# One of five dense token blocks computed mixed: gathered dots on VectorE during the front, its weights through the gate matrices into the dense second stage

## The chip, the cores and the metric

The kernel runs on one core of a Trainium2 chip. TensorE (PE in the profile, PEld for its weight loads) multiplies matrices, VectorE (DVE) and ScalarE (ACT) work elementwise, GpSimd (POOL) does elementwise work and issues the indirect transfers, SyncE (SP) issues most other transfers. The metric is the device time of one execution in microseconds (us), as the median of several runs; lower is better.

## The reference, cut to what matters

The input is 1024 tokens of 1024 features, f32. A mixer (mLSTM heads and gated MLP groups) adds to the residual x; then a PEER layer looks up 16 of 16384 single-neuron experts for each of 8 heads of each token:

```python
q = (xt @ w_query).reshape(T, PEER_HEADS, 2, PEER_HALF)
s = jnp.einsum('thpd,hpkd->thpk', q, sub_keys)
...                     # top 16 of each half, top 16 of their sums: idx and gate (T, 8, 16)
ub = jnp.take(expert_u, ib, axis=0)      # per block of 128 tokens
vb = jnp.take(expert_v, ib, axis=0)
a = jax.nn.gelu(jnp.einsum('td,thkd->thk', xb, ub))
return jnp.einsum('thk,thkd->td', a * gb, vb)
```

So every token has 128 picks: a dot product with a row of `u` for each, a gelu, a gate, and a weighted sum of rows of `v`. A final RMSNorm follows.

## The kernel before, in words

The tokens are 8 blocks of 128. The PEER layer treats them in two ways.

**Dense blocks 0 to 4** (`DENSE`, line 28). All 16384 experts are computed for all 640 tokens, 128 experts (one expert row) at a time. Stage 1 (`stage1` in `experts`, lines 768 to 791) multiplies the row of `uT` with the transposed activations `xh`/`xl`; every product is made of three float32r matmuls of high and low halves (`mm3`, lines 89 to 96). With 8 chunks of 128 features and two halves of 320 tokens that is 48 matmuls of 320 columns for one row. ACT applies the gelu (L786), DVE multiplies with the gate matrix `Gin` (L788), ACT and DVE split the result into `wh` and `wl` (L789, L790). Stage 2 (`stage2`, lines 793 to 814) runs once per group of four rows (`GS`): for each of 5 blocks and 2 halves of the features it accumulates 12 matmuls of 512 columns into `pout`, and DVE adds that to `acc` (L814). POOL makes the low halves of `u` and `v` (L779, L801), ACT the high ones (L778, L800). There are 32 groups.

The gate matrices are made ahead, by `gate_units` (lines 641 to 666): 32 "quads" a block, each one compare on DVE (L656), four scaled copies on ACT (L659), four f32 matmuls (L661, each is two records) and a copy out on ACT (L662); every eighth quad stores 2 MB to `d_G`. Stage 1 reads `d_G` back once per group as `Gin` (one buffer, L771).

**Sparse blocks 5 to 7** (`SPARSE`). For each block `sparse_units` gathers one row of `u` per token with an indirect transfer (POOL, L693) and takes its dot product on DVE (L697), 128 times; then the same with rows of `v`, added into an accumulator (L709, L713). That is 768 gathers of 512 KB. They go into 4 buffers `gat` and, in the dense part, 3 more under the tag `AB`. Their instructions are emitted between the expert rows of the dense loop, in even portions (`SPREAD`, line 833).

**The front** (`front_part`) makes everything ahead of that, in three parts of 2, 3 and 3 blocks (`PARTS`): mixer, output projection, the normalised activations (high and low halves of the dense blocks stored to `d_xh`, `d_xl`, and loaded in `open_x`), the queries and scores. Top-k work (`topk_units`) and gate matrices of one part's blocks are side work of the next part: `interleave` emits it among the steps of `front_part`, spread over the first 210 of a nominal 332 units (`FTOT`). So the gate matrices of blocks 0 and 1 are side work of part 1, those of blocks 2 to 4 of part 2.

**What sets the order.** The kernel is written in Tile. A simulated timeline at build time gives each engine one fixed instruction order, by priority (`first()` raises some evictions) and expected readiness; on the chip each engine and each DMA queue takes its instructions strictly in that order, with semaphore waits. Gathers in the dense part are held in program order on POOL (`keep_in_program_order`).

Of the kernel before, what the change touches and what calls it, by code (L numbers as in the profile page):

```python
# [18 lines left out]
D = 1024  # L19
# [7 lines left out]

DENSE = [0, 1, 2, 3, 4]
SPARSE = [5, 6, 7]
GS = 4  # L30
# [9 lines left out]
NRAW = 3  # L40
NGAT = 4
SLOW = 0
# [4 lines left out]
class Build:  # L47
# [405 lines left out]
    def topk_units(self, blk):  # L453
# [15 lines left out]
        def merge(h0):  # L469
            ijg = st["ijg"]  # L470
            self.merge16(h0, st["tv"], st["ti"], ijg)
            if blk in self.sparse:
                if h0 == 0:
                    self.pick[blk] = (self.kp.tile([128, 128], I32, name="ix", tag=f"ix{blk % 2}"),
                                      self.kp.tile([128, 128], F32, name="gt", tag=f"gt{blk % 2}"))
                ix, gt = self.pick[blk]
                hl = slice(h0 * 16, (h0 + HB) * 16)
                v.scalar_tensor_tensor(ix[:, hl], ijg[:, 0, hl], float(NEXP), ijg[:, 1, hl], op0=OP.mult, op1=OP.add)
                v.tensor_copy(gt[:, hl], ijg[:, 2, hl])

        def done():
            ijg = st["ijg"]
            if blk in self.dense:
                pt = self.gps.tile([128, 3, 128], F32, name="pG", tag="pG", bufs=2)
                for k in range(3):
                    nc.tensor.transpose(pt[:, k], ijg[:, k], self.ident)
                t = self.gp.tile([128, 3, 128], F32, name="ijgT", tag="ijgT", bufs=1)
                nc.scalar.activation(t, pt, AF.Copy)
                self.pick[blk] = t
# [68 lines left out]
    def front_part(self, part):  # L558
# [115 lines left out]


    def sparse_units(self, blk, pool, psum):

# [3 lines left out]
        def begin():  # L681
            st["ix"], st["gt"] = self.pick[blk]
            st["xn"] = psum.tile([128, D], F32, name="xn", tag="xn", bufs=1)
# [54 lines left out]
    def open_x(self):  # L738

        nc = self.nc  # L740
        self.cm.close()
        self.xp = self.ctx.enter_context(self.tc.tile_pool(name="xparts", bufs=1, side="right", reuse_waits="tile"))
        T = len(self.dense) * 128
        self.xh = self.xp.tile([128, 8, T], F32R, name="xh", tag="xh")
        self.xl = self.xp.tile([128, 8, T], F32R, name="xl", tag="xl")
        for s, blk in enumerate(self.dense):
            for src, dst in ((self.d_xh, self.xh), (self.d_xl, self.xl)):
                nc.sync.dma_start(dst[:, :, s * 128:(s + 1) * 128].bitcast(F32), src[blk])
# [7 lines left out]
    def experts(self, side, dp, ps):  # L756
# [4 lines left out]
        ND = len(self.dense)  # L761
        T = ND * 128
        T2 = T // 2
        n32 = T // TG
        ngroups = NEXP // GS
        W, V, st = {}, {}, {"n": 0}

        def stage1(g, e):
            if e == 0:
                st["G"] = dp.tile([128, n32, GS, TG], F32, name="Gin", tag="Gin", bufs=1)  # L770
                nc.sync.dma_start(st["G"], self.d_G[:, :, g * GS:(g + 1) * GS].rearrange("n j i t -> j n i t"))  # L771
            G = st["G"]
            i = g * GS + e
# [7 lines left out]
            wl = dp.tile([128, T], F32R, name="wl", tag="wl", bufs=GS + 1)  # L781
            for s in range(2):
                pa = ps.tile([128, T2], F32, name="pa", tag="pa", bufs=3)
                sl = slice(s * T2, (s + 1) * T2)
                self.mm3(pa, [((uh[:, c], ul[:, c]), (xh[:, c, sl], xl[:, c, sl])) for c in range(8)])
                nc.scalar.activation(pa, pa, AF.Gelu_apprx_tanh)  # L786
                p3 = pa.rearrange("p (n t) -> p n t", t=TG)
                v.tensor_tensor(p3, p3, G[:, s * (n32 // 2):(s + 1) * (n32 // 2), e], op=OP.mult)  # L788
                nc.scalar.activation(wh[:, sl], pa, AF.Copy)  # L789
                v.tensor_sub(wl[:, sl], pa, wh[:, sl].bitcast(F32))  # L790
            W[i] = (wh, wl)

        def stage2(g):
# [9 lines left out]
            for s in range(ND):  # L803
                for d in range(2):
                    if st["n"] % 3 == 0:
                        po = ps.tile([128, 512], F32, name="pout", tag="pout", bufs=1)
                    else:
                        po = self.gps.tile([128, 512], F32, name="pout", tag="pG", bufs=2)
                    st["n"] += 1
                    dl = slice(d * 512, (d + 1) * 512)  # L810
                    sl = slice(s * 128, (s + 1) * 128)
# [51 lines left out]
    def side_units(self, b0, nb):  # L863

        side, prev = [], []
        for blk in range(b0, b0 + nb):
            if blk in self.dense:
                if blk != b0:
                    side += merged(prev, self.topk_units(blk))
                prev = self.gate_units(blk)  # L870
        return side + prev

    def run(self):
        tc = self.tc
        ND = len(self.dense)
        with ExitStack() as ctx:
# [13 lines left out]
            self.kp = ctx.enter_context(tc.tile_pool(name="keep", bufs=1))  # L890
            self.pick = {}
            self.ctx = ctx
# [104 lines left out]
```

## Time and profile before

| | us |
|---|---|
| median of 3 runs | 2883.05 (2881.18 to 2901.98) |
| profiled execution | 2879.65 |
| its span, first to last instruction | 2877.8 |
| part 0 of the front, about | 0 to 228 |
| part 1, about | 228 to 585 |
| part 2, about | 585 to 985 |
| dense loop, with the sparse blocks inside it | 1005 to 2820 |
| end | 2820 to 2878 |

The parts are read from the first and last instructions of lines that belong to one step (the load of x at 230 and 560, the query evictions up to 976, the first stage 1 at about 1000). Of 2877.8 us PE is busy for 2708.7, DVE 2195.1, POOL 1501.2 and ACT 1120.9. A busy share is no rate: matmul records overlap, so the pace of PE is read from the distance between the starts of two matmuls.

### The profile page before, as it was taken

The numbers are of one execution on the slowest core, as the hardware profiler recorded it, in microseconds if no ns is written. First come the engines' busy times: TensorE is split into PE (matmuls) and PEld (weight loads), VectorE is DVE, ScalarE is ACT, GpSimd is POOL, SyncE is SP. The second block draws the span as 40 slices with busy tenths as digits, with TensorE's granted clock in tenths as the row PEclk, the third lists the DMA queues.
The fourth block names the chain that finished last, engine by engine and source line by source line (L and its number), as shares of the span: only waits on it lengthen the run. The fifth ranks groups of instructions, "written<-read, shape, count | busy, mean of one in ns | idle before, by whom it ended". The sixth has DMA issues, their size and how long they took to land.

```text
span 2877.8 us, 44768 instructions
## 1 busy us (share of the span) xinstructions
PE 2708.7 (94%) x16283; PEld 2470.3 (86%) x16283; DVE 2195.1 (76%) x4981; ACT 1120.9 (39%) x2295; POOL 1501.2 (52%) x1220
## 2 busy tenths in 40 slices
PE   7888989999898799999989999999999999999998
PEld 7887989889898798888878889889888899888987
DVE  6649975289985677888887787978987777777774
ACT  5444788348888332223222222223222232222222
POOL 3430010000100186777766677767767777768772
PEclk9989999999999899999999999999999999999999
DMA  7798557866578798998988999998889999989992
GB/s 245 256 313 281 188 211 280 276 223 225 187 272 302 264 326 300 323 336 306 333 288 304 336 321 331 308 342 308 309 280 331 344 327 332 334 314 332 326 345 95
DMA packets 327821, 838.41 MB, mean 291 GB/s; under 512 B 25520, under 2 KB 161072, under 8 KB 315824
## 3 DMA queue, kind: packets, MB, share of 16 engines
q0 software_dynamic: 114048, 427.87, 40.2%
q1 hardware_dynamic: 190544, 347.91, 37.5%
q10 hardware_dynamic: 23008, 59.77, 5.3%
q8 instruction: 128, 2.10, 0.3%
q14 instruction: 93, 0.76, 0.1%
HBM read 746.32 MB, written 89.13 MB: 290 GB/s over the span
## 4 chain that ended last, share of the span: by engine, by line
PE 58%; DVE 17%; DMA 9%; issue 6%; ACT 4%; POOL 4%; SPq 1%; ACTq 1%; POOLq 0%; DVEq 0%
PE pa L96 7%; PE pa L94 7%; PE pa L95 7%; PE pout L94 7%; PE pout L95 7%; PE pout L96 7%; DMA Gin<-d_G 3%; PE pG L661 3%; DVE sacc L713 2%; DVE gat L697 2%; PE pq L94 2%; PE pq L96 1%; PE pq L95 1%; DVE AB L656 1%; DMA raw<-v 1%
## 5 line engine op out<-in xcount | busy, mean ns | idle before, releaser
L94 PE MATMUL pa<-xh,uhi 128*128 128x320 f32 x2048 | 639.7, 312 | 42.2 <-DVE wl L790 26.4
L95 PE MATMUL pa<-xl,uhi 128*128 128x320 f32 x2048 | 637.3, 311 | 0.0
L96 PE MATMUL pa<-xh,ulo 128*128 128x320 f32 x2048 | 626.3, 312 | 4.2 <-POOL ulo L779 3.9
L94 PE MATMUL pout<-vhi,wh 128*128 128x512 f32 x1280 | 503.5, 398 | 17.4 <-DVE acc L814 15.4
L713 DVE SCALAR_TENSOR_TENSOR sacc<-gat,aw,sacc 128x1024 f32<-128x1024 f32 x384 | 492.3, 1282 | 30.6 <-DMA gat<-v,ix 22.8
L95 PE MATMUL pout<-vlo,wh 128*128 128x512 f32 x1280 | 507.4, 398 | 0.0
L709 POOL DMA_INDIRECT gat<-v,ix x384 | 364.3, 949 | 240.7 <-DVE sacc L713 140.0
L96 PE MATMUL pout<-vhi,wl 128*128 128x512 f32 x1280 | 488.5, 398 | 0.0
L693 POOL DMA_INDIRECT gat<-u,ix x384 | 365.5, 952 | 202.6 <-DVE gat L697 102.3
L697 DVE SCALAR_TENSOR_TENSOR gat<-gat,xn 128x1024 f32<-128x1024 f32 x384 | 459.5, 1212 | 15.3 <-DMA gat<-u,ix 15.1
L94 PEld LDWEIGHTS pa<-xh,uhi 128*128 128x128 f32 x2048 | 389.6, 190 | 56.1 <-DVE wl L790 30.7
L96 PEld LDWEIGHTS pa<-xh,ulo 128*128 128x128 f32 x2048 | 386.1, 190 | 11.1 <-POOL ulo L779 7.1
L95 PEld LDWEIGHTS pa<-xl,uhi 128*128 128x128 f32 x2048 | 389.6, 190 | 6.9
L779 POOL TENSOR_TENSOR ulo<-raw,uhi 128x1024 fp32r<-128x1024 f32 x128 | 309.0, 2416 | 144.0 <-ACT uhi L778 142.1
L800 ACT ACTIVATE vhi<-raw 128x1024 fp32r<-128x1024 f32 x128 | 131.8, 1052 | 504.4 <-PE pout L95 442.3
L801 POOL TENSOR_TENSOR vlo<-raw,vhi 128x1024 fp32r<-128x1024 f32 x128 | 307.9, 2416 | 34.1 <-ACT vhi L800 31.7
L94 PEld LDWEIGHTS pout<-vhi,wh 128*128 128x128 f32 x1280 | 241.7, 189 | 73.7 <-DVE acc L814 19.2
L814 DVE TENSOR_TENSOR acc<-acc,pout 128x512 f32<-128x512 f32 x320 | 214.5, 682 | 109.1 <-PE pout L96 96.0
L95 PEld LDWEIGHTS pout<-vlo,wh 128*128 128x128 f32 x1280 | 242.2, 189 | 50.6 <-POOL vlo L801 0.4
L96 PEld LDWEIGHTS pout<-vhi,wl 128*128 128x128 f32 x1280 | 240.2, 189 | 52.8
L788 DVE TENSOR_TENSOR pa<-pa,Gin 128x320 f32<-128x320 f32 x256 | 126.6, 494 | 202.2 <-ACT pa L786 108.0
L789 ACT ACTIVATE wh<-pa 128x320 fp32r<-128x320 f32 x256 | 111.8, 437 | 423.7 <-DVE pa L788 340.7
(243 smaller groups left out, 5039.4 us busy)
## 6 DMA issues: line engine op xcount, KB each, us to landing
raw<-uT SPq DMA_DIRECT2D x128, 512.0 KB
raw<-v SPq DMA_DIRECT2D x128, 512.0 KB
wlo<-d_wl SPq DMA_DIRECT2D x48, 1024.0 KB
d_G<-Gt ACTq DMA_DIRECT2D x20, 2048.0 KB
Gin<-d_G SPq DMA_DIRECT2D x32, 1280.0 KB
wraw<-win SPq DMA_DIRECT2D x72, 512.0 KB
d_wl<-wlo POOLq DMA_DIRECT2D x24, 1024.0 KB
wraw<-wq SPq DMA_DIRECT2D x48, 512.0 KB
```

The lines of the kernel that those rows point to most:

```text
L94: te.matmul(ps, lh, rh, start=k == 0, stop=False)
L95: te.matmul(ps, lh, rl, start=False, stop=False)
L96: te.matmul(ps, ll, rh, start=False, stop=k == n - 1)
L693: gd = nc.gpsimd.indirect_dma_start(out=t, out_offset=None, in_=self.I["u"], in_offset=bass.IndirectOffsetOnAxis(ap=st["ix"][:, k:k + 1], ...
L697: v.scalar_tensor_tensor(t, t, 1.0, st["xn"], op0=OP.mult, op1=OP.mult, accum_out=st["a"][:, k:k + 1])
L709: gd = nc.gpsimd.indirect_dma_start(out=t, out_offset=None, in_=self.I["v"], in_offset=bass.IndirectOffsetOnAxis(ap=st["ix"][:, k:k + 1], ...
L713: v.scalar_tensor_tensor(st["acc"], t, st["a"][:, k:k + 1], st["acc"], op0=OP.mult, op1=OP.add)
L779: nc.gpsimd.tensor_tensor(ul, ur, uh.bitcast(F32), op=OP.subtract)
L788: v.tensor_tensor(p3, p3, G[:, s * (n32 // 2):(s + 1) * (n32 // 2), e], op=OP.mult)
L800: nc.scalar.activation(vh, vr, AF.Copy)
L801: nc.gpsimd.tensor_tensor(vl, vr, vh.bitcast(F32), op=OP.subtract)
L814: v.tensor_add(st["acc"][:, s, dl], st["acc"][:, s, dl], po)
```

## The change

Block 0 leaves the dense first stage and stays in the second. `MIXED` names it. Its picked indices and gates are kept (`slots`, as for a sparse block). The new `dot_units` gathers its `u` rows into two buffers (`drow`) and takes the 128 dot products on DVE; then gelu, gate, and a transpose put the finished weights in the place of the gates in `pick`. `gate_units` of block 0 then scatters weights, not gates, so its slices of `d_G` hold the second stage's operand itself. In the dense loop these slices are split into `mh` and `ml` once per group, on ACT and POOL, and stage 2 takes them for block 0. Stage 1 has 512 tokens in one piece. The first 88 of the units (`EARLY`: the start and 87 dots) are side work of part 1, merged with block 1's top-k and gates; the other 41 dots, the end and block 0's 32 quads are side work of part 2, merged with that part's own. `gat` gets a fifth buffer.

```diff
+MIXED = 0
+EARLY = 88
-NGAT = 4
+NGAT = 5
@@ topk_units, merge and done
-            if blk in self.sparse:
+            if blk in self.sparse or blk == MIXED:
...
-                for k in range(3):
+                n = 2 if blk == MIXED else 3
+                for k in range(n):
                     nc.tensor.transpose(pt[:, k], ijg[:, k], self.ident)
@@ front_part
-            if blk in self.dense:
+            if blk in self.dense[1:]:
                 bl = slice(b * 128, (b + 1) * 128)
                 nc.scalar.dma_start(self.d_xh[blk], self.ah[:, :, bl].bitcast(F32))
@@ new
+    def dot_units(self, blk):
...
+        def row():
+            return self.fp.tile([128, D], F32, name="drow", tag="drow", bufs=2)
+
+        def begin():
...
+            nc.sync.dma_start(st["xn"], self.d_x1[blk])
+            g2 = row()
+            nc.sync.dma_start(g2, self.I["n2row"].partition_broadcast(128))
+            v.scalar_tensor_tensor(st["xn"], st["xn"], self.rall[:, blk:blk + 1], g2, op0=OP.mult, op1=OP.mult)
+
+        def dot(k):
+            t = row()
+            ix = self.slots[blk][0]
+            gd = nc.gpsimd.indirect_dma_start(out=t, out_offset=None, in_=self.I["u"],
+                                              in_offset=bass.IndirectOffsetOnAxis(ap=ix[:, k:k + 1], axis=0))
+            self.tc.keep_in_program_order(gd)
+            v.scalar_tensor_tensor(t, t, 1.0, st["xn"], op0=OP.mult, op1=OP.mult, accum_out=st["a"][:, k:k + 1])
+
+        def end():
+            a = st["a"]
+            nc.scalar.activation(a, a, AF.Gelu_apprx_tanh)
+            v.tensor_mul(a, a, self.slots[blk][1])
+            pt = self.gps.tile([128, 128], F32, name="pG", tag="pG", bufs=2)
+            nc.tensor.transpose(pt, a, self.ident)
+            nc.scalar.activation(self.pick[blk][:, 2], pt, AF.Copy)
+
+        return [begin] + [lambda k=k: dot(k) for k in range(128)] + [end]
@@ experts, stage1
+                m = st["M"] = tuple(dp.tile([128, GS, 128], F32R, name=n, tag=n, bufs=2) for n in ("mh", "ml"))
...
+                nc.scalar.activation(mh, src, AF.Copy)
+                nc.gpsimd.tensor_tensor(ml, src, mh.bitcast(F32), op=OP.subtract)
...
-            for s in range(2):
-                pa = ps.tile([128, T2], F32, name="pa", tag="pa", bufs=3)
-                sl = slice(s * T2, (s + 1) * T2)
-                self.mm3(pa, [((uh[:, c], ul[:, c]), (xh[:, c, sl], xl[:, c, sl])) for c in range(8)])
...
+            pa = ps.tile([128, T], F32, name="pa", tag="pa", bufs=3)
+            self.mm3(pa, [((uh[:, c], ul[:, c]), (xh[:, c], xl[:, c])) for c in range(8)])
+            nc.scalar.activation(pa, pa, AF.Gelu_apprx_tanh)
+            p3 = pa.rearrange("p (n t) -> p n t", t=TG)
+            v.tensor_tensor(p3, p3, G[:, m32:, e], op=OP.mult)
+            nc.scalar.activation(wh, pa, AF.Copy)
+            v.tensor_sub(wl, pa, wh.bitcast(F32))
@@ stage2
-                    self.mm3(po, [((W[i][0][:, sl], W[i][1][:, sl]), (V[i][0][:, dl], V[i][1][:, dl]))
-                                  for i in range(g * GS, (g + 1) * GS)])
+                    part = [[x[:, i % GS] if s == 0 else y[:, sl] for x, y in zip(M[g], W[i])]
+                            for i in range(g * GS, (g + 1) * GS)]
...
@@ side_units
+                prev = [] if blk == MIXED else self.gate_units(blk)
+        side += prev
+        if b0 <= MIXED < b0 + nb:
+            dots = self.dot_units(MIXED)
+            self.left = dots[EARLY:] + self.gate_units(MIXED)
+            return merged(dots[:EARLY], side)
+        side, self.left = merged(side, self.left), []
+        return side
```

## Rows read from the trace of the kernel before

**Rows 1.** The page: busy tenths of the DMA engines and GB/s, in 40 slices.
```profile
DMA  7798557866578798998988999998889999989992
GB/s 245 256 313 281 188 211 280 276 223 225 187 272 302 264 326 300 323 336 306 333 288 304 336 321 331 308 342 308 309 280 331 344 327 332 334 314 332 326 345 95
```

**Rows 2.** Stretches: busy us (instructions) by engine, granted clock, DMA share, GB/s.
```profile
228.00:585.00 357.00, 327.19 (x2309) 307.91 (x2310) 246.19 (x895) 236.77 (x567) 30.13 (x45) 0.97 0.68 243
585.00:985.00 400.00, 363.01 (x2605) 344.19 (x2603) 318.91 (x1162) 288.59 (x723) 24.18 (x34) 0.97 0.68 239
...
1005.00:2820.00 1815.00, 1766.17 (x9675) 1584.63 (x9674) 1450.45 (x2486) 467.70 (x770) 1325.39 (x1017) 0.99 0.91 320
```

**Rows 3.** Groups by line, engine PE: shape, count, busy us, mean ns, idle before.
```profile
L95 PE MATMUL pa<-xl,uhi 128*128 128x320 f32 x2048 | 637.3, 311 | 0.0
...
L94 PE MATMUL pout<-vhi,wh 128*128 128x512 f32 x1280 | 503.5, 398 | 17.4 <-DVE acc L814 15.4 <-issue 1.4 <-ACT wh L789 0.6
```

**Rows 4.** Order of time, PE, start us, duration us; four and five matmuls left out between.
```profile
1701.01 0.31 PE L94 MATMUL pa<-xh,uhi 128*128 128x320 f32 x1
...
1701.74 0.31 PE L96 MATMUL pa<-xh,ulo 128*128 128x320 f32 x1
1701.89 0.39 PE L94 MATMUL pout<-vhi,wh 128*128 128x512 f32 x1
...
1703.28 0.40 PE L94 MATMUL pout<-vhi,wh 128*128 128x512 f32 x1
```

**Rows 5.** Stretches of the dense loop, columns as in group 2.
```profile
1320.00:1340.00 20.00, 20.00 (x101) 17.15 (x100) 15.44 (x32) 2.25 (x4) 13.10 (x11) 1.00 1.01 356
1640.00:1660.00 20.00, 20.00 (x106) 17.55 (x106) 19.35 (x35) 5.14 (x9) 13.78 (x13) 1.00 1.00 391
1460.00:1480.00 20.00, 16.57 (x76) 14.38 (x77) 18.71 (x31) 7.52 (x10) 10.52 (x8) 0.83 0.58 177
2300.00:2400.00 100.00, 100.00 (x573) 91.55 (x573) 76.50 (x140) 27.92 (x47) 80.83 (x61) 1.00 0.94 329
```

**Rows 6.** Groups by line and shape, engine DVE.
```profile
L697 DVE SCALAR_TENSOR_TENSOR gat<-gat,xn 128x1024 f32<-128x1024 f32 x384 | 459.5, 1212 | 15.3 <-DMA gat<-u,ix 15.1
L814 DVE TENSOR_TENSOR acc<-acc,pout 128x512 f32<-128x512 f32 x320 | 214.5, 682 | 109.1 <-PE pout L96 96.0 <-issue 11.7 <-PE pout L94 1.0
L656 DVE TENSOR_TENSOR AB<-iota,ijgT 128x1024 f32<-128x1024 f32 x160 | 195.7, 1229 | 59.6 <-PE pG L661 48.2 <-ACT sc L446 5.7 <-ACT whi L77 1.6
L788 DVE TENSOR_TENSOR pa<-pa,Gin 128x320 f32<-128x320 f32 x256 | 126.6, 494 | 202.2 <-ACT pa L786 108.0 <-DMA Gin<-d_G 55.9 <-issue 28.5
L790 DVE TENSOR_TENSOR wl<-pa,wh 128x320 fp32r<-128x320 f32 x256 | 123.8, 484 | 34.8 <-ACT wh L789 26.9 <-issue 7.1 <-ACT uhi L778 0.8
...
L697 DVE DVE_READ_ACCUMULATOR gat<-gat,xn 128x1 f32 x384 | 31.4, 82 | 0.0
```

**Rows 7.** Groups by line and shape, engine ACT.
```profile
L659 ACT ACTIVATE AB<-AB,ijgT 128x128 f32<-128x128 f32 x640 | 203.0, 396 | 36.5 <-DVE AB L656 25.0 <-DMA xh<-d_xh 10.3 <-DVE s L553 0.4
...
L662 ACT ACTIVATE Gt<-pG 128x512 f32<-128x512 f32 x160 | 93.0, 588 | 27.0 <-PE pG L661 26.2
```

**Rows 8.** Groups by line and shape, engine POOL.
```profile
L693 POOL DMA_INDIRECT gat<-u,ix x384 | 365.5, 952 | 202.6 <-DVE gat L697 102.3 <-issue 58.4 <-DVE gt L479 6.5
...
L779 POOL TENSOR_TENSOR ulo<-raw,uhi 128x1024 fp32r<-128x1024 f32 x128 | 309.0, 2416 | 144.0 <-ACT uhi L778 142.1
```

**Rows 9.** Stretch of part 2 in which side work is densest, columns as in group 2.
```profile
600.00:700.00 100.00, 97.54 (x677) 89.79 (x676) 95.39 (x411) 68.01 (x156) 6.72 (x11) 1.00 0.62 216
```

**Rows 10.** One line, L656: duration min/median/max, first and last start.
```profile
L656 DVE TENSOR_TENSOR AB<-iota,ijgT x160: 1187/1219/1898, 309.4 to 937.1; 128x1024 f32<-128x1024 f32 x160
```

**Rows 11.** Chain of waits, two places: start us, us, what.
```profile
1130.02 6.83 DMA gat<-u,ix
...
2610.55 7.03 DMA gat<-v,ix
```

**Rows 12.** Waits, engine DVE, dense loop: waited for, us in total, times, longest.
```profile
DVE pa L788 <- DMA Gin<-d_G: 55.9, 10, 9.5
```

More of the change, by code (lines that the diff above doesn't have):

```diff
@@ L484, in done @@
                 pt = self.gps.tile([128, 3, 128], F32, name="pG", tag="pG", bufs=2)
-                for k in range(3):
+                n = 2 if blk == MIXED else 3
+                for k in range(n):
                     nc.tensor.transpose(pt[:, k], ijg[:, k], self.ident)
-                t = self.gp.tile([128, 3, 128], F32, name="ijgT", tag="ijgT", bufs=1)
-                nc.scalar.activation(t, pt, AF.Copy)
+                t = self.gp.tile([128, 3, 128], F32, name="ijgT", tag="ijgM" if blk == MIXED else "ijgT", bufs=1)
+                nc.scalar.activation(t[:, 0:n], pt[:, 0:n], AF.Copy)
                 self.pick[blk] = t
@@ L742, in open_x @@
         self.xp = self.ctx.enter_context(self.tc.tile_pool(name="xparts", bufs=1, side="right", reuse_waits="tile"))
-        T = len(self.dense) * 128
+        T = (len(self.dense) - 1) * 128
         self.xh = self.xp.tile([128, 8, T], F32R, name="xh", tag="xh")
         self.xl = self.xp.tile([128, 8, T], F32R, name="xl", tag="xl")
-        for s, blk in enumerate(self.dense):
+        for s, blk in enumerate(self.dense[1:]):
             for src, dst in ((self.d_xh, self.xh), (self.d_xl, self.xl)):
@@ L761, in experts @@
         ND = len(self.dense)
-        T = ND * 128
-        T2 = T // 2
-        n32 = T // TG
+        T = (ND - 1) * 128
+        n32 = ND * 128 // TG
+        m32 = 128 // TG
         ngroups = NEXP // GS
-        W, V, st = {}, {}, {"n": 0}
+        W, V, M, st = {}, {}, {}, {"n": 0}
         def stage1(g, e):
@@ L781, in stage1 @@
             wl = dp.tile([128, T], F32R, name="wl", tag="wl", bufs=GS + 1)
[L782 to L791 removed]
+            pa = ps.tile([128, T], F32, name="pa", tag="pa", bufs=3)
[5 more added lines that the diff above has]
+            v.tensor_sub(wl, pa, wh.bitcast(F32))
+            W[i], M[g] = (wh, wl), st["M"]
         def stage2(g):
@@ L810, in stage2 @@
                     dl = slice(d * 512, (d + 1) * 512)
-                    sl = slice(s * 128, (s + 1) * 128)
-                    self.mm3(po, [((W[i][0][:, sl], W[i][1][:, sl]), (V[i][0][:, dl], V[i][1][:, dl]))
-                                  for i in range(g * GS, (g + 1) * GS)])
+                    sl = slice((s - 1) * 128, s * 128)
+                    part = [[x[:, i % GS] if s == 0 else y[:, sl] for x, y in zip(M[g], W[i])]
+                            for i in range(g * GS, (g + 1) * GS)]
+                    self.mm3(po, [(w, (V[i][0][:, dl], V[i][1][:, dl]))
+                                  for w, i in zip(part, range(g * GS, (g + 1) * GS))])
                     v.tensor_add(st["acc"][:, s, dl], st["acc"][:, s, dl], po)
@@ L890, in run @@
             self.kp = ctx.enter_context(tc.tile_pool(name="keep", bufs=1))
[L891 removed]
+            self.pick, self.slots = {}, {}
             self.ctx = ctx
```

15 lines of the change are left out of this document (10 added, 5 removed).

## The prediction

> **What bounds the kernel now.** I read the stretches first [rows 2]. The dense loop, 1815 of 2877.8 us, is the largest, and there PE is busy for 1766 us. But busy time says little, because matmul records overlap: a 320-column one is given 311 ns [rows 3], while the starts move by 0.73 us over five of them, 0.146 us each, and by 1.39 us over six of 512 columns, 0.232 us each [rows 4]. Both are 0.453 to 0.456 ns a column, so inside a burst PE is paced by columns and nothing else. Counted so, the loop's 3 x 2048 = 6144 narrow matmuls and 3 x 1280 = 3840 wide ones [rows 3] need 6144 x 0.146 + 3840 x 0.232 = 897 + 891 = 1788 us. With the last stage 2, which runs past 2820, that is nearly all of the loop: PE sets its pace. The rest follows closely. In a steady hundred microseconds PE is full at the full clock, DVE is at 76, POOL at 81, and the DMA engines at 0.94 with 329 GB/s [rows 5].
>
> The front is another machine. In parts 1 and 2 DMA is at 0.68, POOL nearly idle (30 and 24 us), and DVE has 246 us of work in 357 and 319 in 400 [rows 2]. Where the side work is densest, in part 2, DVE is at 95 of 100 us [rows 9]. So the change takes work from a full PE in the loop and gives work to a DVE that has about 110 us to spare in part 1 and 80 in part 2.
>
> **Stage 1, the gain.** 48 matmuls of 320 columns a row become 24 of 512: 128 x 24 = 3072, at 0.232 us 713 us in place of 897, so 184 us less PE time. That 512 columns cost what the sum says is seen in stage 2, which has that shape already. The row's evictions shrink too: DVE's two passes are 126.6 + 123.8 = 250 us now [rows 6]; 256 passes of 512 columns at L814's 682 ns are 175, so 75 us less. ACT loses little and is no bound. Stage 2 keeps its 3840 matmuls.
>
> **Stage 2's new operand.** 32 splits of block 0's slices: ACT 32 x 0.59 us (L662, the same 512 elements [rows 7]), POOL 32 x 1.2 us, half of L779's 2.4 us [rows 8], 39 us on an engine with 1325 us of work in 1815 [rows 2]. The price is zero at best; at worst these wait at the head of POOL and ACT for the one buffer `Gin`, with the gathers and `ulo` queued behind. DVE waits there today, 55.9 us over 10 times [rows 12], so at most about 56 us more. I take nothing extra, since it is the same landing that DVE already waits for and the row's `pa` buffers now hold three rows, not one and a half. Its cover is POOL's remaining idle time.
>
> **What keeps the loop from giving back all 184 us.** Its data do not shrink: 320 GB/s x 1815 us = 581 MB [rows 2], almost all gathers, `u` and `v`. In 1815 - 184 = 1631 us that is 356 GB/s. Ends: short stretches carry 356 and even 391 GB/s at a share of 1.0 [rows 5], by which nothing is lost and the gain is 184; a steady stretch carries 329 to 331 at 0.94, and at 331 the loop needs 1755 us, a gain of 60. The best slices of 72 us hold 342 to 345 [rows 1]. I take 342, which lies between and is the longest stretch above the steady one: 581 / 0.342 = 1699 us, **a gain of 116**. DVE (1450 - 75 = 1375 us) and POOL (1325 + 39 = 1364) are then at 80 of 100, as in steady stretches today, so neither binds before DMA. When PE does pause, its clock falls, as in the 20 us where it was busy for 16.6 and the granted clock was 0.83, a third of that time at 1.2 GHz instead of 2.4 [rows 5]; in a loop paced by DMA that costs nothing further.
>
> **The front, the price.** One dot is 1.212 + 0.082 = 1.29 us on DVE [rows 6] and 0.95 us on POOL [rows 8]; one quad is 1.23 us on DVE [rows 6] and 4 x (203.0 / 640) + 0.59 = 1.86 us on ACT [rows 7].
>
> Part 1 gets 87 dots (112 us of DVE) and loses block 0's 32 quads (39 us of DVE, 59 of ACT, and 8 records each on PE): DVE goes from 246 to 319 us in 357. That fits, and PE and ACT are relieved. I take no change; ends -30 (PE and ACT relief, were DVE's order no limit) and +40. The gathers' 46 MB bring the part from 243 to about 370 GB/s less the 8 MB of gate matrices that leave it, about 350: the weight loads lose their spare bandwidth, which is the upper end.
>
> Part 2 gets 41 dots (53 us) and the 32 quads (39 us): DVE 319 + 92 = 411 us in 400. It can't be hidden. At the 95 of 100 that DVE reaches in its fullest stretch [rows 9], 411 us take 433, so +33. By the quads' own pace the price is higher: block 2 to 4's 96 quads ran from about 660 to 937 [rows 10], 2.89 us each, and 32 more would add 92. I take **+40**, near the first, because quads wait for each other's buffers and dots fill these gaps. Lowest +11 (DVE at 100). Late first in the next stage is the first `Gin`, which needs all the gate matrices.
>
> Small edits: `ix`, `gt`, the start and the end are some ten short DVE and ACT instructions and three f32 transposes fewer or more, beside other work, 0 to 5 us. Two activation stores and two loads of 512 KB go; nothing waits for them. On SP two loads are added ahead of part 1's weight loads, 1 MB, under 3 us by the steady rate. A fifth `gat` buffer can only let gathers run further ahead.
>
> **The gathers in the front** have only two buffers. A gather that DVE waited for took 6.83 and 7.03 us to land in the loop [rows 11]; with 0.95 for the issue and 1.29 for the dot, two buffers give a dot every (0.95 + 6.9 + 1.29) / 2 = 4.6 us, so 128 dots take 585 us, from about 309 (when block 0's first quads run now [rows 10]) to 894, and block 0's quads come after that. This is just in time for a gate store that ended near 937. So the chain alone adds little to the +40, if DVE's fixed order puts each dot where its row has landed. Where it does not, DVE waits with the front's evictions queued behind, and so does POOL, where a gather that waits for a buffer stands ahead of the small rstd and gating steps of the front.
>
> By the Trainium skill's page "DMA: Bandwidth & Descriptors", section "Anatomy of one DMA — SWDGE (gpsimd) path", a transfer costs 2.0 us plus its bytes over 436 GB/s, an estimate of 3.2 us for 512 KB. By that a dot would come every 2.7 us and the chain would end near 660; the trace's landings are twice as long, in a loop where DMA is at 0.91.
>
> **The sum.** 2879.65 (the profiled execution, 3.4 us below the median) - 116 + 0 + 40 = 2804 us.
>
> **Rivals.** (1) *The forecast*: DMA holds the loop at about 342 GB/s, part 2 grows by DVE's overflow: 2804. Chance 0.45; its own range, with the ends of part 1 and part 2 and the loop at 338 to 350 GB/s, is 2765 to 2850.
> (2) *The loop stays bound by PE*: it takes all 184, front as above: 2736. The 391 GB/s stretch [rows 5] speaks for it; against it, no slice of 72 us is above 345. Chance 0.12.
> (3) *The front is free*: part 1 gives up what part 2 adds, 2879.65 - 116 = 2764. For it, ACT's relief; against it, DVE's sums. Chance 0.08.
> (4) *DMA gives no more than now in steady stretches*, 331 GB/s: 2879.65 - 60 + 40 = 2860, no change that counts. For it, the DMA share is 0.94 with a full PE, and the `raw` loads of `u` and `v` must land within a shorter row. Chance 0.18.
> (5) *Slower: the waits for gathered rows sit in DVE's order in the front.* Place: L697's counterpart ahead of the front's evictions. Each of 128 dots can wait up to 4.6 - 1.29 = 3.3 us, 420 us in all. The loop's gain less the front's 40 is 76 us, so at 0.6 us a dot nothing is left, and above 0.84 us (108 us) the kernel is slower by over 1%. At a third of the bound, 1.1 us, it is 140 us: 2879.65 - 116 + 40 + 140 = 2944. For it: two buffers, and an order fixed by a simulated timeline. Against it: that order spreads the dots over 600 us. Chance 0.17.
> That the change does not do what it says is excluded for its main term by the 512-column pace [rows 4].
>
> About 1% (2854 to 2912 us) is what a measurement of this kernel tells from no change. Faster: nearly all of (1), (2) and (3), 0.65. Same: (4) and the edge of (1), 0.18. Slower: (5), 0.17. Range 2745 to 2895: it holds (1), (3), (4) and the milder half of the others.
>
> **What would show it.** In the loop: `pa` matmuls 0.232 us apart, half as many; 72 us slices at 340 GB/s or more with DMA at 0.97 or above, and PE waiting for DVE's `wl` or for `ulo` more than now. If the slices stay at 330, (4); if PE is full and they reach 355, (2). In the front: part 1's end still near 585, the first stage 1 near 1040 instead of 1000. A sum of waits of DVE for `drow` above 75 us shows (5). Wrong altogether would be a loop no shorter than 1755 us, or a start of the loop after 1120.

## The result: slower, by a front that grew five times as much as forecast

The kernel after takes 3023.01 us (median of 4 runs, 3010.24 to 3031.29) against 2882.11 before, a ratio of 1.0466 [1.0426, 1.0506]. The forecast was 2804. The profiled execution took 3019.86, its span is 3018.1.

Two rows split it, the first and last start of stage 2's matmuls. Before:

```profile
L94 PE MATMUL pout<-vhi,wh x1280: 388/395/797, 1010.8 to 2867.0; 128*128 128x512 f32 x183
```

After, the same line (now L96):

```profile
L96 PE MATMUL pout<-vhi,wh x1024: 387/396/796, 1214.7 to 2923.7; 128*128 128x512 f32 x171
```

The first `pout` starts 203.9 us later: that is the front's price. (Stage 1 of the first group began at 1016.7, where it was 992.0 before, but after 72 matmuls, three rows, PE stood still until the gate matrices came. So "loop start" here is the first `pout`.) PE's own loop shrinks from 1856.2 to 1709.0 us (-147.2). From the last `pout` to the end of the span there were 10.8 us and now there are 94.4 (+83.6). So loop and tail together give 63.6. 2879.65 + 203.9 - 63.6 = 3020.

The stretches of after, columns as in [rows 2]:

```profile
228.00:585.00 357.00, 314.25 (x2069) 293.01 (x2068) 264.54 (x940) 190.14 (x416) 91.23 (x96) 0.93 0.83 297
585.00:985.00 400.00, 333.93 (x2193) 308.52 (x2193) 341.37 (x1239) 212.20 (x492) 112.02 (x103) 0.91 0.80 287
985.00:1205.00 220.00, 118.50 (x700) 105.86 (x700) 131.98 (x208) 142.38 (x398) 41.76 (x29) 0.79 0.46 178
1205.00:2925.00 1720.00, 1635.02 (x6840) 1298.23 (x6840) 1326.99 (x2179) 426.07 (x556) 1305.35 (x988) 0.98 0.90 319
2925.00:3018.00 93.00, 0.00 (x0) 0.00 (x0) 83.65 (x67) 6.86 (x12) 57.19 (x64) 0.51 0.87 335
```

DVE has done not 411 us of work in part 2 but 341, because part of the quads has slipped behind it: a stretch of 220 us has appeared behind it in which no engine is busy for more than two thirds of the time and PE's granted clock is 0.79. The last 93 us have no matmul at all. In the loop DMA still moves 319 GB/s, as before.

The page's slices answer to [rows 1]: no plateau at 340 or more, and the gap before the loop is plain.

```profile
DMA  7798779988689445899998988989889989999988
GB/s 252 256 332 299 256 267 352 307 295 294 231 298 325 171 159 209 310 318 324 327 327 312 320 294 311 356 315 345 309 303 330 318 287 331 314 330 318 322 325 335
```

What the front was doing shows in three lines: the last query eviction (the end of the front's own chain), the dots, and the quads, which answer to [rows 10].

```profile
L433 ACT ACTIVATE qk<-pq x48: 363/472/493, 178.6 to 973.7; 128x384 f32<-128x384 f32 x32, 128x256 f32<-128x256 f32 x16
L700 DVE SCALAR_TENSOR_TENSOR drow<-drow,dxn x128: 1192/1216/1858, 253.9 to 1010.5; 128x1024 f32<-128x1024 f32 x128
L659 DVE TENSOR_TENSOR AB<-iota,ijgT x160: 1199/1219/3384, 399.9 to 1177.9; 128x1024 f32<-128x1024 f32 x160
```

The front's own chain ends at 974, as before (976). The side work does not: the dots end at 1010, the quads at 1178 where they ended at 937. Quads on DVE by stretches of 50 us (DVE busy, instructions, granted clock, DMA share, GB/s):

```profile
950.00:1000.00 50.00, 0.00 (x0) 0.78 0.68 229
1000.00:1050.00 50.00, 18.28 (x14) 0.84 0.48 178
1050.00:1100.00 50.00, 30.52 (x27) 0.90 0.36 134
1100.00:1150.00 50.00, 26.14 (x22) 0.76 0.38 161
1150.00:1200.00 50.00, 16.89 (x14) 0.76 0.51 203
```

No quad runs between 950 and 1000, and 75 run after it (one that crosses a border counts in both stretches). In the time order of DVE they follow directly on the last dot (1010.47):

```profile
1010.47 1.23 DVE L700 SCALAR_TENSOR_TENSOR drow<-drow,dxn 128x1024 f32<-128x1024 f32 x1 [1.38 <-DMA drow<-u,ix]
1011.62 0.08 DVE L700 DVE_READ_ACCUMULATOR drow<-drow,dxn 128x1 f32 x1
1012.08 0.29 DVE L705 TENSOR_TENSOR daw<-daw,gt 128x128 f32<-128x128 f32 x1 [0.38 <-ACT daw L704]
1014.65 1.23 DVE L659 TENSOR_TENSOR AB<-iota,ijgT 128x1024 f32<-128x1024 f32 x1 [2.28 <-PE pG L664]
```

PE's longest single wait of the front is the transpose of the finished weights (`daw`), which shares the buffers `pG` with the quads (waited for, us in total, times, longest):

```profile
PE pG L707 <- DVE daw L705: 37.0, 1, 37.0
```

### The profile page after: what moved, and what is told of

It reads as the page before. It is cut to its first block, busy times and chain, and to the rows that moved or that the text cites. A ratio compares the mean times of both kernels' runs of the same rounds, so it can differ in the third digit from the quotient of the medians.

```text
span 3018.1 us, 38746 instructions
## 1 busy us (share of the span) xinstructions
PE 2594.4 (86%) x13211; PEld 2186.0 (72%) x13211; DVE 2288.5 (76%) x4987; ACT 1085.3 (36%) x2075; POOL 1702.0 (56%) x1380
## 4 chain that ended last, share of the span: by engine, by line
PE 40%; DVE 21%; DMA 15%; issue 11%; POOL 7%; ACT 5%; ACTq 1%; SPq 1%; another core or an unknown queue 0%; POOLq 0%; DVEq 0%
PE pout L97 6%; PE pout L98 6%; PE pout L96 6%; DMA Gin<-d_G 5%; DVE gat L734 4%; PE pa L98 3%; PE pa L96 3%; PE pa L97 3%; DMA drow<-u,ix 3%; DVE sacc L750 2%; POOL vlo L842 2%; ACT AB L662 2%; DVE AB L659 2%; POOL gat L746 2%; DVE drow L700 1%
## 5 line engine op out<-in xcount | busy, mean ns | idle before, releaser
L750 DVE SCALAR_TENSOR_TENSOR sacc<-gat,aw,sacc 128x1024 f32<-128x1024 f32 x384 | 493.1, 1284 | 31.0 <-DMA gat<-v,ix 25.1
L96 PE MATMUL pout<-vhi,wh 128*128 128x512 f32 x1024 | 413.4, 404 | 31.8 <-DVE acc L857 26.2
L697 POOL DMA_INDIRECT drow<-u,ix x128 | 150.5, 1176 | 470.6 <-DVE drow L700 204.6
L96 PE MATMUL pa<-xh,uhi 128*128 128x512 f32 x1024 | 408.4, 399 | 6.8 <-ACT uhi L821 4.4
L97 PE MATMUL pout<-vlo,wh 128*128 128x512 f32 x1024 | 410.3, 401 | 0.0
L98 PE MATMUL pa<-xh,ulo 128*128 128x512 f32 x1024 | 402.3, 397 | 6.0 <-POOL ulo L822 6.0
L97 PE MATMUL pa<-xl,uhi 128*128 128x512 f32 x1024 | 406.7, 397 | 0.0
L664 PE MATMUL pG<-AB 128*128 128x128 f32 x1280 | 202.3, 309 | 66.2 <-ACT Gt L665 44.9
L96 PEld LDWEIGHTS pout<-vhi,wh 128*128 128x128 f32 x1024 | 196.0, 191 | 86.2 <-DVE acc L857 32.5
L664 PEld LDWEIGHTS pG<-AB 128*128 128x128 f32 x1280 | 185.0, 214 | 80.8 <-ACT Gt L665 51.9
L659 DVE TENSOR_TENSOR AB<-iota,ijgT 128x1024 f32<-128x1024 f32 x160 | 195.1, 1237 | 57.8 <-PE pG L664 29.6
L96 PEld LDWEIGHTS pa<-xh,uhi 128*128 128x128 f32 x1024 | 193.5, 189 | 57.7 <-ACT uhi L821 8.3
L98 PEld LDWEIGHTS pa<-xh,ulo 128*128 128x128 f32 x1024 | 192.7, 188 | 54.6 <-POOL ulo L822 8.2
```

The source lines that it names most:

```text
L96: te.matmul(ps, lh, rh, start=k == 0, stop=False)
L97: te.matmul(ps, lh, rl, start=False, stop=False)
L98: te.matmul(ps, ll, rh, start=False, stop=k == n - 1)
L659: nc.vector.tensor_tensor(AB, self.iota[:, None, None, :].to_broadcast([128, 2, 4, 128]), t3[:, 0:2, t0:t0 + 4, None].to_broadcast([128, 2 ...
L664: nc.tensor.matmul(pg[:, u], AB[:, 1, u], AB[:, 0, u], start=True, stop=True)
L750: v.scalar_tensor_tensor(st["acc"], t, st["a"][:, k:k + 1], st["acc"], op0=OP.mult, op1=OP.add)
```

## Experiments on the front

"Loop start" is the first `pout` of `wh`. "Behind" is how many of the 160 quads stand behind the last dot in DVE's built order. All ratios are to the kernel before.

| kernel | us | ratio | last dot | behind | last quad | loop start | last `pout` | end of span |
|---|---|---|---|---|---|---|---|---|
| before | 2882.1 | 1 | - | - | 937.1 | 1010.8 | 2867.0 | 2877.8 |
| after | 3023.0 | 1.0466 [1.0426, 1.0506] | 1010.5 | 75 | 1177.9 | 1214.7 | 2923.7 | 3018.1 |
| e3_no_dots | 2801.1 | 0.9702 [0.9651, 0.9753] | - | - | 921.7 | 995.9 | 2697.0 | 2801.2 |
| e14_nogather | 2889.7 | 1.0014 [0.9987, 1.0040] | 538.1 | 140 | 1046.9 | 1084.1 | 2782.8 | 2875.5 |
| e4_drow1 | 3299.5 (one run) | - | 1286.0 | 75 | 1451.6 | 1488.7 | 3206.1 | 3297.7 |
| e8_drow3 | 2988.3 | 1.0365 [1.0288, 1.0442] | 882.1 | 96 | 1152.6 | 1190.0 | 2897.8 | 2989.3 |
| e7_early130 | 3075.2 | 1.0654 [1.0585, 1.0723] | 919.6 | 128 | 1222.9 | 1260.4 | 2970.0 | 3064.1 |
| e1_quads_last | 2973.2 | 1.0269 [1.0211, 1.0326] | 1062.5 | 29 | 1127.8 | 1167.8 | 2890.5 | 2979.1 |
| e11, quads last, EARLY 129 | 2940.5 | 1.0208 [1.0150, 1.0267] | 1036.8 | 29 | 1102.7 | 1139.1 | 2856.2 | 2935.5 |

**e3_no_dots: the dense half alone.**

```
-  prev = [] if blk == MIXED else self.gate_units(blk)
+  prev = self.gate_units(blk)          # and no dot_units; n = 3 in topk_units
```

> Leaves out block 0's gathered dots, its gelu and its products: its second-stage weights are the gates alone; its quads run in part 1 as in the kernel before. The loop is that of the changed kernel. If the front's loss is all from the dots and the quads behind them: the loop starts near 1005 as before, and the loop with its tail takes what it took in the changed kernel, 1813 us, total about 2820. If the loop gives what was forecast (116 less than before): 2764. If the loop's tail was caused by the late start of the sparse stream: 2740.

2801.12, a ratio of 0.9702. The loop starts at 995.9, so the quads alone are as early as before, and all of the loss is the dots and what they push. Loop and tail last 2801.2 - 995.9 = 1805.3 us, as in the kernel after (1803.4): what the loop gives does not depend on the front.

**e14_nogather: the dots without their gathers.**

```
-  t = row(); gd = nc.gpsimd.indirect_dma_start(out=t, ...)
-  v.scalar_tensor_tensor(t, t, 1.0, st["xn"], ...)
+  t = row()                            # bufs=1, output only
+  v.scalar_tensor_tensor(t, st["row"], 1.0, st["xn"], ...)   # one fixed tile
```

> The changed kernel without the 128 gathers in the front: every dot takes the same row tile, loaded once, so the dots' values are wrong and their DVE work is the same. If the gather chain through the buffers is what delays the loop: the dots end early, the loop starts near 1010 to 1045, total 2800 to 2850, and block 0's quads hold nobody. If the dots' DVE work in a front whose DVE is nearly full is what costs: the loop starts after 1120, total above 2920.

```profile
L698 DVE SCALAR_TENSOR_TENSOR drow<-drowf,dxn x128: 1150/1212/3484, 175.4 to 538.1; 128x1024 f32<-128x1024 f32 x128
L659 DVE TENSOR_TENSOR AB<-iota,ijgT x160: 1193/1217/3519, 475.2 to 1046.9; 128x1024 f32<-128x1024 f32 x160
```

2889.66, level with the kernel before. The loop starts at 1084.1. That lies between its two forecasts (up to 2850, and above 2920), so neither theory holds alone. Between e3 and this stand 88 us for DVE's 128 dots and the quads that start after them; between this and the kernel after 131 us (1084.1 to 1214.7), or 133 of the medians, for the gathers. The split is a rough one, since each build has an order of its own: here the dots end at 538 and 140 quads follow them, 3.6 us each. Even with no gather this order only breaks even.

**e4_drow1 and e8_drow3: the chain of gathers.** One and three buffers in place of two (with three, `NRAW = 2` makes room for it).

```
-  name="drow", tag="drow", bufs=2
+  name="drow", tag="drow", bufs=1      # e8: bufs=3
```

> One drow buffer in place of two; the build leaves DVE's order as it is. If the chain issue, landing, dot, release through two buffers sets the 5.9 us per dot: one buffer gives 8 to 10 us per dot, the last dot near 1300 to 1500 instead of 1010, total 3300 or more. If the places of the dots in DVE's order set the pace (the gathers mostly wait for DVE to come to a dot whose row has landed): the last dot moves by less than 100 us, total under 3120.

> Three drow buffers instead of two, paid for with two wraw buffers instead of three. If the chain through the buffers sets the pace (8.1 us a dot with one, 5.9 with two): 4.5 to 5 us with three, last dot near 860, loop start near 1080 to 1130, total 2900 to 2950, less what the lost wraw buffer costs. If DVE's fixed order sets the pace with two already: last dot within 50 us of 1010, total 3000 or more.

The dots run at 8.1 us each with one buffer ((1286.0 - 249.8) / 128), 5.9 with two ((1010.5 - 253.9) / 128) and 4.8 with three ((882.1 - 271.8) / 128). So the number of buffers does set when the dots end, close to what both runs forecast. With one buffer the profile also gives the landing of a gather, counted from the start of its issue:

```profile
DMA to landing us min/median/max: 4.1/4.6/13.6
```

With one buffer the whole kernel shifts with the last dot: last dot +275.5, loop start +274.0. With three the last dot is 128 us earlier, but the loop starts only 25 us earlier, at 1190 where 1080 to 1130 was forecast: now 96 quads stand behind the dot, not 75, and the last query eviction has gone from 974 to 1067. What is taken from the chain comes back as a longer queue of quads and a later main chain; how much of the latter is due to the `wraw` buffer that was given up for it, this run does not tell.

**e7_early130: all dots in part 1's portion.**

```
-EARLY = 88
+EARLY = 130
```

> All 130 dot units are side work of part 1; only the quads of block 0 are left to part 2. If the chain of dots is late because its last third was emitted only in part 2: the last dot comes before 850 us instead of 1010, the loop starts near 1040 instead of 1212, total 2850 to 2880. If DVE's load in part 1 is the limit (246 - 39 + 166 = 373 us of work in 357): the last query eviction moves from 974 to beyond 1010 and the total stays above 2940.

```profile
850.00:900.00 50.00, 0.00 (x0) 1.00 0.95 363
900.00:950.00 50.00, 12.66 (x7) 0.80 0.62 214
950.00:1000.00 50.00, 22.67 (x19) 0.77 0.30 116
...
1150.00:1200.00 50.00, 27.00 (x23) 0.86 0.44 168
```

(Quads on DVE in 50 us, as above.) The dots end 91 us earlier and the loop starts 46 us later. Here 128 quads stand behind the last dot, those of blocks 2 to 4 among them, which ran from about 660 on in the kernel before. They run at about the pace of the kernel after, some 22 in 50 us. Both forecasts fail: the dots end later than 850, and the last query eviction comes not after 1010 but at 903, 70 us earlier than in the kernel after.

**e1_quads_last and e11: block 0's quads put behind all others.**

```
-  self.left = dots[EARLY:] + self.gate_units(MIXED)
+  self.left, self.last = dots[EARLY:], self.gate_units(MIXED)
-  side, self.left = merged(side, self.left), []
+  side = merged(side, self.left) + self.last      # e11: also EARLY = 129
```

> Block 0's 32 quads are emitted after all other side work of part 2, not merged with it; 29 quads, not 75, stand behind the last dot in DVE's order. Theory A (the quads of blocks 3 and 4 stand behind block 0's in the shared rotating buffers, and these wait for the last dot at 1010 us): 46 quads of about 2.1 us move ahead of it, the loop starts near 1105 instead of 1205, total about 2920 us. Theory B (DVE has more side work than fits ahead of 1010, whatever the order): the loop still starts near 1200, total 3005 to 3035.

> All 128 dots are side work of part 1; the end unit (gelu, gate, transpose through the shared PSUM tile pG) and then block 0's quads are emitted after all other side work of part 2. Theory A (what takes a buffer of the quads in program order and waits for the last dot holds every quad behind it; that is the end unit's pG and block 0's quads): the quads of blocks 2 to 4 run while the dots go on, only 32 follow the last dot (919 us in the run with all dots early, perhaps 950 here), loop start 1030 to 1075, total 2830 to 2885. Rival (the front's engines are full, DVE above all, and any order gives about the same): loop start after 1130, total above 2930.

In e1, 46 quads leave the queue behind the last dot, the dots end 52 us later, and the loop starts 47 us earlier, between its two forecasts (1105 and 1200). e11, with all dots but the end unit in part 1, starts another 29 earlier. Its 1139 and 2940 us are what its rival forecast, a front whose engines are full: the last dot comes not near 950 but at 1037, and the last query eviction has gone from 974 to 1017 (1026 in e1). So the order is worth 76 us here, and the other 143 down to e3's 996 stay. In the built order of e11's edit with EARLY = 130 (not run) 128 quads stand behind again, though it differs from e11 only in where the end unit is emitted: its transpose takes a buffer `pG`, and block 0's quads behind it take `AB`, `Gt` and `pG` in turn, so that quads of other blocks that follow them in emission can't pass. In the kernel after, e1, e4, e7 and e11 the last quad starts 2.2 to 2.4 us per quad behind the last dot, and the loop some 37 us later. With 2.25 and 35 us: 1010.5 + 75 x 2.25 + 35 = 1214 for the kernel after (1214.7), 1062.5 + 29 x 2.25 + 35 = 1163 for e1 (1167.8), 919.6 + 128 x 2.25 + 35 = 1243 for e7 (1260.4). These numbers were fitted to these runs. They hold only for quads that run behind the main chain: where they run beside it, a quad takes 2.8 us (e8) and 3.6 us (e14).

## Experiments on the loop

From the loop's start to the end of the span it is 1867 us before and 1803 after, where the forecast was 116 less than before. What ends last has changed. From the loop's start to their last add the sparse blocks take 1811 us before and 1793 after, hardly less, while PE's own loop shrinks by 147: before, PE's last `pout` came 45 us after that add, now it comes 84 us before it. Of the 84 us that DVE works in the tail, 73 are `L750`, the adds of the sparse blocks: 57 of them stand behind the last add of `acc`, where before there was none. The line of before (L713), then two of after:

```profile
L713 DVE SCALAR_TENSOR_TENSOR sacc<-gat,aw,sacc x384: 1251/1281/1292, 1307.8 to 2822.2; 128x1024 f32<-128x1024 f32 x192
```

```profile
L750 DVE SCALAR_TENSOR_TENSOR sacc<-gat,aw,sacc x384: 1254/1283/1318, 1497.1 to 3007.9; 128x1024 f32<-128x1024 f32 x192
L857 DVE TENSOR_TENSOR acc<-acc,pout x320: 665/682/690, 1218.8 to 2927.8; 128x512 f32<-128x512 f32 x160
```

| kernel | us | ratio | loop start | last `pout` | end | start to end |
|---|---|---|---|---|---|---|
| e5_pin | 3014.0 | 1.0443 [1.0375, 1.0511] | 1214.1 | 2998.9 | 3011.4 | 1797 |
| e6_nodots_pin | 2805.9 | 0.9711 [0.9647, 0.9775] | 1000.2 | 2796.5 | 2807.2 | 1807 |
| e2_m_late | 2995.7 | 1.0370 [1.0322, 1.0417] | 1209.2 | 2913.0 | 2994.2 | 1785 |
| e10, half of `u` | 2784.9 | 0.9660 [0.9607, 0.9714] | 988.8 | 2769.9 | 2780.6 | 1792 |
| e12, less DVE | 2808.2 | 0.9740 [0.9705, 0.9775] | 995.4 | 2794.0 | 2804.7 | 1809 |
| e13, less POOL | 2805.8 | 0.9730 [0.9695, 0.9765] | 996.3 | 2790.8 | 2801.5 | 1805 |
| e9, POOL to DVE | 2903.1 | 1.0063 [1.0034, 1.0093] | 999.9 | 2876.5 | 2887.2 | 1887 |

**e5_pin and e6_nodots_pin: the order that makes the tail.** The first `acc` add of a group is held in program order with the gathers (e6 is e3 with this).

```
-  v.tensor_add(st["acc"][:, s, dl], st["acc"][:, s, dl], po)
+  t = v.tensor_add(st["acc"][:, s, dl], st["acc"][:, s, dl], po)
+  if (s, d) == (0, 0):
+      self.tc.keep_in_program_order(t)
```

> The changed kernel with one edit: the first add into acc of every group is pinned on DVE behind the sparse work emitted before it, so that no add of a sparse block stands behind the last acc in DVE's order (57 before). Theory T (the 84 us after PE's last matmul are laid down in that order, 1.4 to 1.5 us an add, not by what the chip can carry): PE's loop, first to last pout, stays within 1700 to 1735 us, the tail falls to about 12 us, total 2940 to 2960. Theory D (POOL and the DMA engines can't carry the gathers any faster): the loop grows by what the tail loses, total 3005 to 3030.

> Leaves out block 0's gathered dots, its gelu and its products, and pins acc as in the run before. Theory T: 2801 us less about 80 = 2720. Theory D: 2790 to 2810. The difference to the pinned kernel with dots is then what the front costs, about 220 us.

The tail goes (94 to 12 us, and 104 to 11 against e3), and PE's loop grows by as much: 1709 to 1785, and 1701 to 1796. Neither time moves by more than its interval. So the order of these adds decides only where the 80 us lie, not whether they are paid; that it alone loses them is refuted.

**e2_m_late: the split of block 0's slices moved from the head of a group to its end.**

```
-  nc.scalar.activation(mh, src, AF.Copy); nc.gpsimd.tensor_tensor(ml, ...)   # e == 0
+  if e == GS - 1:  # at the end of stage1
+      nc.scalar.activation(mh, src, AF.Copy); nc.gpsimd.tensor_tensor(ml, ...)
```

> The split of block 0's slices into mh and ml is emitted at the end of a group's fourth row, not at its start. Theory P (POOL stands for 102 us at ml, waiting for mh and so for Gin, with gathers queued behind; that is why the gathers end 85 us after PE): POOL's wait at ml falls under 20 us, the tail after PE's last matmul shrinks to 30 us or less, total 2940 to 2970 us. Theory T (the tail is laid down by DVE's fixed order, in which 57 adds stood behind the last acc, now 49, or by the DMA rate): tail about 75 us, total 3005 to 3020.

POOL's waits in the loop (1210 to 2925), first after, then e2:

```profile
POOL ml L814 <- ACT mh L813: 102.3, 19, 10.9
```

```profile
POOL ml L833 <- ACT mh L832: 53.6, 11, 8.5
```

27 us less in the median, 18 of them between loop start and end. Neither forecast is met: POOL's wait falls to 53.6 and not below 20, and the tail is still 81 us. The split that was priced at nothing costs at least this much where it stands: POOL waits 102 us for it, with gathers and `ulo` queued behind, and half of this can be had back. The price is that of this kernel: in e13 below, without the dots, leaving out `ml` and a quarter of the `vl` gives nothing.

**e10, e12, e13: one resource at a time, all on e6.** e10 loads `u` only for even rows (33.5 MB less); e12 computes `wl` once per group; e13 computes `ml` once and three `vl` of four.

```
e10:  if i % 2 == 0: st["ur"] = self.raw()...; nc.sync.dma_start(st["ur"], self.I["uT"][i])
e12:  if e == 0: v.tensor_sub(wl, pa, wh.bitcast(F32))
e13:  if g == 0: nc.gpsimd.tensor_tensor(ml, ...)
      if e < 3: nc.gpsimd.tensor_tensor(vl, ...)     # else vl = vls[:, 2]
```

> Leaves out block 0's dots, gelu and products, acc pinned; and half of the loads of uT are left out (odd rows use the row before), 33.5 of the loop's 581 MB. ACT's and POOL's work on them stays. Theory D (DMA): 33.5 MB at 323 to 340 GB/s, total 2700 to 2715 against 2806. Theory Q (POOL): under 25 us less, total 2780 to 2806.

> Leaves out block 0's dots, gelu and products, acc pinned; and the low half wl is computed for one row of each group and used for all four: 96 passes of 0.68 us, 65 us less on DVE. If DVE's sequence carries the loop: 50 to 90 us less, total 2715 to 2755 against 2806. If another engine does: less than 20 us, total 2785 or more.

> Leaves out block 0's dots, gelu and products, acc pinned; and POOL makes ml once and three vlo of four (the fourth matmul set uses the third's): 115 us less on POOL, nothing added elsewhere, and POOL no longer stands at ml. If POOL's queue carries the loop: 60 to 110 us less, total 2695 to 2745. If DVE does: less than 25 us, total 2780 or more. If each waits for the other in turn (coupled queues): 30 to 60 us in both this run and the one before.

The loop of e6, then of e12, e13 and e10, columns as in [rows 2]:

```profile
1000.00:2796.00 1796.00, 1665.41 (x6834) 1298.22 (x6833) 1407.87 (x2250) 433.74 (x563) 1369.23 (x1056) 0.97 0.90 324
```

```profile
1000.00:2796.00 1796.00, 1664.80 (x6818) 1302.11 (x6817) 1359.15 (x2147) 430.42 (x560) 1362.66 (x1053) 0.97 0.91 323
```

```profile
1000.00:2796.00 1796.00, 1652.94 (x6822) 1294.85 (x6821) 1405.21 (x2249) 432.63 (x564) 1249.95 (x994) 0.97 0.90 323
```

```profile
989.00:2770.00 1781.00, 1664.03 (x6852) 1300.71 (x6852) 1419.04 (x2260) 429.84 (x564) 1367.99 (x1058) 0.97 0.88 308
```

DVE with 49 us less and POOL with 119 us less give nothing. Queues that wait for each other in turn were to give 30 to 60 us in both runs; that is not met either. 33.5 MB less, which at the loop's 324 GB/s is 103 us of transfers, give 21 us in the medians (the intervals of the ratios overlap) and 15 from loop start to end; e10 also holds each tile of `u` for two rows, which can cost some of its gain. So neither DVE's nor POOL's work nor the bytes of `u` pace the loop by themselves. Nor does the landing of the gathers: in e3, by the landing semaphores in the trace, a row lands on average 6.2 us after its issue, then waits 5.8 us for its place in DVE's order, and the freed buffer waits about 4.6 us for POOL's next gather. More buffers, or gathers in another order, were not tried. What PE waits for in e6 (1000 to 2820) is spread over three engines:

```profile
PE pout L96 <- DVE acc L857: 43.7, 41, 5.4
PE pout L97 <- POOL vlo L842: 42.5, 36, 3.0
PE pout L96 <- ACT vhi L841: 24.5, 12, 8.7
```

**e9: POOL's `ml` and every fourth `vl` given to DVE, on e6.**

```
-  nc.gpsimd.tensor_tensor(ml, ...)
+  v.tensor_tensor(ml, ...)
-  nc.gpsimd.tensor_tensor(vl, ...)
+  t = (v if e == 3 else nc.gpsimd).tensor_tensor(vl, ...)   # DVE's held in program order
```

> Leaves out block 0's dots, gelu and products, acc pinned as before; and POOL loses 115 us of work: the split ml and every fourth vlo go to DVE (about 70 us more there). Theory Q (POOL's queue is what now carries the loop: 1368 us of work, 127 us between gathers and 200 us of waits in 1790): the loop shortens by 60 to 110 us, total 2700 to 2745 against 2806 for the same kernel without this edit. Theory D (the DMA engines carry it, at 323 GB/s): total 2790 to 2815.

97 us slower than e6, outside both forecasts, though DVE is busy for only 1495 us of 1876. PE now waits for POOL and ACT, and POOL waits for DVE to free gather buffers (`PE`: 1000 to 2820; `POOL`: 1000 to 2880):

```profile
PE pa L98 <- POOL ulo L822: 81.0, 42, 5.1
PE pa L96 <- ACT uhi L821: 41.1, 20, 5.8
```

```profile
POOL gat L746 <- DVE sacc L750: 146.7, 141, 9.0
POOL gat L730 <- DVE gat L734: 115.3, 116, 4.7
```

These waits read as DVE's work reaching PE by way of POOL's queue: a gather that waits for its buffer holds the `ulo` behind it. The run also gives the moved work a fixed place in DVE's order, and does not separate the two.

## Why the prediction was wrong, step by step

**The failed step is the front: "This is just in time for a gate store that ended near 937. So the chain alone adds little to the +40, if DVE's fixed order puts each dot where its row has landed."** The front cost 204. Two things in that step failed.

*A buffer's turn was longer than issue, landing and dot.* The forecast's 4.6 us a dot is half of a turn of 0.95 + 6.9 + 1.29 = 9.1 us. It measured 5.9 a dot, so the dots, though they began at 254 and not at 309, ended at 1010 and not at 894, 117 us later. The landing semaphores in the trace (the events that tell that a transfer has arrived) split the turn of the 128 gathers, on average: 1.2 us issue, 5.9 from its end to the landing, 2.8 in which the landed row waits for its dot in DVE's order, 1.2 for the dot, 0.9 until POOL issues the next gather into the buffer; 12.0 in all. (About one event in thirty is missing there.) So the landing was shorter than forecast, and what the forecast put at nothing were the two waits, 3.7 us a turn. The waits of the engines say the same: POOL waited 204.6 us for DVE to free `drow`, DVE only 57.8, at 27 of the 128 dots, for rows.

```profile
  DMA drow<-u,ix: 57.8, 27
who waited for it (us, times):
  POOL drow L697: 204.6, 53
```

By the Trainium skill's page "DMA: Bandwidth & Descriptors", section "Anatomy of one DMA — SWDGE (gpsimd) path", the landing was estimated at 3.2 us. The trace has that only for the quickest gather with one buffer (4.1 us from the start of an issue of 0.94); the mean from the issue's end is 4.7 us with one buffer and 5.9 with two.

*More than block 0's quads stood behind the last dot.* The prediction let 32 quads follow it. 75 did: buffers that turn in emission order let no later quad pass the ones that wait for the dots, and the count follows the emission order in e1 and e11 (29) and in e7 (128). 43 quads more at 2.25 us are 97 us, beside the 117 of the chain. Together that is more than the 164 us by which the front missed its +40, so the two terms name the places and do not add up to a proof: at the same pace the forecast's own 894 and 32 quads would have started the loop at 894 + 72 + 35 = 1001, and not 40 us later than before. Each quad there is paid in full, because the front's own chain has ended: the stretch 985 to 1205 has PE at 118 of 220 us. The chain that ends last there (1005 to 1210) goes through the whole quad, from its copies on ACT to the 2 MB stores of its result, and hardly through DVE:

```profile
by line: ACT AB L662 25.9%; DMA d_G<-Gt 19.0%; PE pG L664 14.7%; ACT Gt L665 11.0%; DMA Gin<-d_G 7.2%; DVE AB L659 5.3%; PE pa L98 2.4%; PE pa L97 2.2%; PE pa L96 2.2%; issue 2.1%; DMA drow<-u,ix 2.1%; DMA acc<-d_x 1.6%; POOL ulo L822 1.6%;
```

Order alone does not cure it. The best one tried (e11) still starts the loop 143 us after e3, with the front's own chain ending 44 us later than in the kernel after; how much of that is DVE's work and how much the chain of gathers, no run separates.

**DVE's overflow, +40,** was too small as well, even with the gathers away: in e14 the loop starts 73 us later than before (88 later than in e3). Part 1 at no change was right for the front's own chain, which ended on time.

**Stage 1's matmuls, -184: right in pace.** Their number halved, and the starts move by 0.233 us (1.40 over six), as [rows 4] let expect:

```profile
2050.43 0.40 PE L96 MATMUL pa<-xh,uhi 128*128 128x512 f32 x1
...
2051.83 0.40 PE L96 MATMUL pa<-xh,uhi 128*128 128x512 f32 x1
```

PE's 6912 matmuls then need 6912 x 0.233 = 1610 us. From the first `pout` to the last it took 1709, of which its waits are 77, on POOL's `vlo` and DVE's `acc` above all.

**The loop, -116 by DMA at 342 GB/s: a size and a mechanism off.** Loop and tail gave 64. That is the number of rival (4), a loop at today's 331 GB/s, but by luck: e10 shows that fewer bytes of `u` hardly help. What PE gives up is not what the loop gives back, because the sparse blocks, hidden behind PE before, still take 1793 us and now end last. What makes them, or the loop as a whole, take about 1800 us in orders that differ as much as e3, e5 and e6 is not the amount of one engine's work, and stays open. Seen, but not shown to set it, are waits of one queue for another (POOL's at `ml`, e2; a gather at the head of POOL's queue, e9); taking work from two engines at once was not tried.

**Block 0's split at nothing: wrong by some 18 to 27 us for its place alone** (e2). Its bound of 56, from DVE's wait at `Gin` [rows 12], was for the wrong wait: that one fell to 26.6 us, but POOL waited 102.3 us for ACT's `mh`, and ACT for `Gin` (393.2 us of idle time, 27 times).

**Rival (5), slower,** named the sign and the place (the dots, in the front) but not the mechanism. It priced DVE waiting for rows: 57.8 us in all, under the 75 that were to show it. In the main it was the rows that waited for DVE. The side work ran late as a queue, with the main chain on time. The prediction's own mark for "wrong altogether", a start of the loop after 1120, is met by the first `pout`, though not by the first stage 1 (1016.7).

## What to carry to other kernels

Side work that is hidden has a deadline, and what has to be summed against it is not only its engine time but its chain (buffers in flight, landing, consumer's order) and everything that shares rotating buffers with its last step. Before work is moved under a cover, count what stands behind it in the fixed order, and multiply by the pace of that work when it has no cover: here 75 x 2.25 us. When a busy engine is relieved, look at what it hides: here a stream of gathers that took almost as long as PE's loop became the end of the kernel as soon as PE was faster.

## What the runs showed of the hardware

- Gathers of 512 KB with one, two and three buffers came every 8.1, 5.9 and 4.8 us, so a second buffer bought 27% and a third 19%. From the end of the issue to the landing semaphore it took 4.7, 5.9 and 6.2 us on average, and the landed row then waited 0.9, 2.8 and 3.2 us for its dot, in a front where DMA is at 0.80 to 0.83 (with two buffers).
- In the 220 us of quads without cover PE, busy for 118 of them, was granted a clock of 0.79, between its two levels of 1.2 and 2.4 GHz; in the loop it had 0.98.
- A loop at 324 GB/s and a DMA share of 0.90 was not held by its bytes alone: 33.5 MB less, 103 us at that rate, shortened it by 15 to 21 us, and the rate fell to 308 GB/s.
